# Three small experts' products placed between the weight units of the five large ones, and the branch for further slots moved behind the experts

## The chip, the core and the metric

The kernel runs on one core of a Trainium2 chip. Its engines run side by side and wait for each other through semaphores: TensorE (PE in the rows, its weight loads PEld), VectorE (DVE), ScalarE (ACT), GpSimd (POOL) and SyncE (SP), which here issues the loads of weights. The metric is the device time of one execution in microseconds, lower is better.

## What is computed

Two transformer blocks of two layers each, over 256 tokens of width 1024, in float32. The change concerns one place, the mixture of experts in the second layer of the first block. A router picks 2 of 8 experts for each token, and each expert is a gated MLP of inner width 3584:

```python
logits = (xt @ w_router).astype(jnp.float32)
top_v, top_e = lax.top_k(logits, TOP_K)
gates = jax.nn.softmax(top_v, axis=-1)
...
def _swiglu(x, w1, w3, w2):
    return (jax.nn.silu(x @ w1) * (x @ w3)) @ w2
```

The output of an expert is scaled by its gate and added to the rows of its tokens.

## The kernel before

All weights go through one `Stream`. A load fetches 1 MiB (128 partitions x 2048 floats) into one of four raw buffers, issued by SP in the order of `Stream.loads`. `Stream.need` (L322 on) splits a raw tile into a high part `wh` (ACT, L338) and a low part `wl` (DVE, L339), each of two k-tiles of 128 rows by 512 columns; six pairs of such buffers exist (`SPLIT_BUFS`). `Thread.gemm` takes a split unit (two k-tiles) and issues three matmuls of 512 columns for each k-tile: L390 and L392 with `wh`, L391 with `wl`. All use the whole array of TensorE, 128 by 128. When a raw tile is split, `Stream.free` issues the next load.

Routing (`routing`) ranks the experts by their number of tokens. The five largest (`BIG`) get 128 slots each and run in `expert128`: for each of seven chunks of 512 inner columns a `gemm` with w1 and one with w3 of 8 k-tiles, then two `gemm` with w2 of 28 k-tiles, which is 42 loads and 3 x (7 x 2 x 8 + 2 x 28) = 504 matmuls for one expert. The inner activations are transposed on PE (L594), and the result is scattered back to the tokens by eight matmuls (L1611, L1612) and added to `XA` on DVE (`add_rows`).

The three smallest experts get 64 slots and run in `expert64` on the raw float32 weights, without splitting. `Thread.gemm_pair` computes two products side by side: a load holds two k-tiles of w1 and two of w3 in two transfers of 512 KB (for w2: two column chunks), and one half of the array's columns takes the first, the other half the second:

```python
for j in range(sk):
    k = k0 + j
    for c in range(2):
        m.nc.tensor.matmul(ps[c * 64:c * 64 + 64, :n], xT(k), w[:, c, j, :], start=(k == 0),
                           stop=(k == kc - 1))
m.stream.free(li)
```

So a load of a small expert is one unit of four matmuls of 64 by 512 (L407), and there are 42 units for each. A float32 matmul shows as two records in the trace. The raw buffer is held until PE has read it.

`moe` runs the eight experts one after the other in the order of ranks 0, 5, 1, 6, 2, 7, 3, 4 (`ORDER`). In the first of them a few loads come as halves into spare tiles (`raws`). `gather` and `gather64` collect an expert's tokens while the one before runs. Ahead of the first expert stands `overflow`: every engine loads the largest excess count into a register and branches (L1672, L1684); its body runs only when an expert has more tokens than slots, and on these inputs it is skipped. After the last expert come a layer norm (BN_AGGR and what follows on DVE) and the second block, which starts with PE transposes of its result.

The order in which instructions stand on each engine is set by a scheduler when the program is built; PE runs its matmuls in that order.

Of the kernel before, what the change touches and what calls it, by code (L numbers as in the profile page):

```python
# [29 lines left out]
SM_N = 2  # L30
SM_END = 7
TOA = 3
TOB = 3
SMALL_AT = 1
# [16 lines left out]
ORDER = (0, 5, 1, 6, 2, 7, 3, 4)  # L51
# [85 lines left out]
def weight_plan():  # L137
# [3 lines left out]
    def add(key, name, idx, c0, c1, small=0):  # L141
        out.append((key, name, idx, c0, c1, small))
# [8 lines left out]
    for i in range(2):  # L151
# [17 lines left out]
        if i == 0:  # L169
            for ci, (a, b) in enumerate(chunks(2816)):  # L170
                add(("f1", ci), "dense_w1", (0,), a, b)
                add(("f3", ci), "dense_w3", (0,), a, b)
            full("f2", "dense_w2", (0,), D)
        else:
            for e in range(8):
                for ci in range(7):
                    small = [SM_N if SMALL_AT <= 7 * e + ci < SM_END else 0 for j in range(2)]
                    add((e, "e1", ci), "expert_w1", (0, e), ci * 512, ci * 512 + 512, small[0])
                    add((e, "e3", ci), "expert_w3", (0, e), ci * 512, ci * 512 + 512, small[1])
                full((e, "e2"), "expert_w2", (0, e), D)  # L180
# [26 lines left out]
def weight_groups(shapes):  # L207
# [5 lines left out]
    for key, name, idx, c0, c1, small in weight_plan():  # L213
# [9 lines left out]
        out.append((key, name, idx, c0, n, kc, small, g))  # L223
# [3 lines left out]
def packed_weights(h):  # L227
# [3 lines left out]
    for key, name, idx, c0, n, kc, small, groups in plan:  # L231
# [4 lines left out]
    return packs  # L236


class Stream:


    def __init__(self, m):
# [7 lines left out]
        self.owed = 0  # L250
        self.pin = True
# [3 lines left out]
    def add(self, key, name, n, kc, small, groups, rank=None):  # L255
        per = part_rows(n)
        lst = []
        for at, k, rows in groups:
            lk = per if len(lst) < small else rows
            for j in range(0, rows, lk):  # L260
                li = len(self.loads)
                self.loads.append(([(name, at, rows, j, lk, n)], lk < rows, rank))
                kk = 0
                while kk < lk:
                    sk = min(per, lk - kk)
                    lst.append(len(self.splits))
                    self.splits.append((li, kk, sk, k + j + kk, n, kc, kk + sk == lk))
                    kk += sk
        assert key not in self.index
        self.index[key] = lst  # L270

    def add_pair(self, key, chunks, kc, rank):

        lst = []
        for g in range(len(chunks[0][2])):
            k, rows = chunks[0][2][g][1:]
            for j in range(0, rows, 2):
                li = len(self.loads)
                self.loads.append(([(name, gr[g][0], rows, j, 2, n) for name, n, gr in chunks], False, rank))
                lst.append(len(self.splits))  # L280
                self.splits.append((li, None, 2, k + j, 512, kc, True))
        assert key not in self.index
        self.index[key] = lst

    def load(self, parts=1):
        while self.next_load < len(self.loads):
            li = self.next_load
            pieces, small, rank = self.loads[li]
            if rank is not None and rank not in self.m.expert:
                self.owed += 1  # L290
                return
            self.next_load += 1
            if small:
                r = self.m.A([P, 1024], F32, name="raws")
            else:
                r = self.m.praw.tile([P, 2048], F32, name="raw", tag="raw")
            for i, (name, at, rows, j0, lk, n) in enumerate(pieces):
                v = r[:, i * lk * n:(i + 1) * lk * n].rearrange("p (k n) -> p k n", k=lk)
                if rank is None:
                    src = self.m.I[name][at:at + P * rows * n].rearrange("(p k n) -> p k n", p=P, k=rows)  # L300
                else:
                    w = self.m.I[name].rearrange("(e q) -> e q", e=8)
                    src = w[bass.ds(self.m.expert[rank], 1), at:at + P * rows * n].rearrange(
                        "a (p k n) -> p (a k) n", p=P, k=rows)
                q = lk // parts
                for j in range(0, lk, q):
                    self.m.nc.sync.dma_start(v[:, j:j + q], src[:, j0 + j:j0 + j + q])  # L307
            self.raw[li] = r if len(pieces) > 1 else v
            if not small:
                return  # L310
# [9 lines left out]

    def need(self, idx):
        m = self.m  # L322
        nc = m.nc
        while self.next_split <= min(idx, len(self.splits) - 1):
            j = self.next_split
            li, kk, sk, k0, n, kc, last = self.splits[j]
            if li not in self.raw:
                return
            self.next_split += 1
            if kk is None:  # L330
                self.ready[j] = self.raw[li].rearrange("p (c k n) -> p c k n", c=2, k=sk)
                continue
# [16 lines left out]
    def free(self, li):  # L349
        del self.raw[li]  # L350
        if not self.loads[li][1]:
            self.load()


class Thread:
# [40 lines left out]
    def gemm_pair(self, key, xT):  # L396

        m = self.m
        ps = m.pmm.tile([P, 512], F32, name="mm", tag="mm")
        for s in m.stream.index[key]:  # L400
            yield s
            li, _, sk, k0, n, kc, _ = m.stream.splits[s]
            w = m.stream.ready.pop(s)
# [15 lines left out]
class Model:  # L419
# [108 lines left out]
    def run_one(self, g):  # L528
        for s in g:
            if isinstance(s, int):  # L530
                self.stream.need(s + SPLIT_BUFS - 2)
                self.stream.next_use = s + 1
                self.side_tick()

# [102 lines left out]
    def plan(self):  # L637
# [3 lines left out]
        for key, name, idx, c0, n, kc, small, groups in weight_groups(SHAPES)[0]:  # L641
            if not name.startswith("expert_"):
                S.add(key, name, n, kc, small, groups)
                continue
            if idx[1] > 0:
                continue
            one[key[1:] if key[1] in ("e1", "e3") else ("e2", key[1])] = (name, n, kc, small, groups)
            if ("e2", 1) not in one:
                continue
            for i, r in enumerate(ORDER):  # L650
                if r < BIG:
                    for k, (nm, nn, kk, sm, gr) in one.items():
                        S.add((r,) + k, nm, nn, kk, sm if i == 0 else 0, gr, r)
                else:
                    for ci in range(8):
                        ab = [one["e1", ci], one["e3", ci]] if ci < 7 else [one["e2", 0], one["e2", 1]]
                        S.add_pair((r, ci), [(nm, nn, gr) for nm, nn, _, _, gr in ab], ab[0][2], r)
# [721 lines left out]
    def routing(self):  # L1379
# [48 lines left out]
        reg(ORDER[0])  # L1428
        self.stream.pay()
        for r in ORDER[1:]:  # L1430
# [29 lines left out]
        yield from self.gather(ORDER[0])  # L1460
# [7 lines left out]
    def gather(self, r):  # L1468
# [3 lines left out]
        s = self.kvt([P, 2, P], name="oh")  # L1472
# [7 lines left out]
        if r == ORDER[0]:  # L1480
# [44 lines left out]
    def gather64(self, r):  # L1525
# [3 lines left out]
        s = self.kvt([P, 2, 2, 64], name="oh")  # L1529
# [9 lines left out]
        sT = []  # L1539
        for h in range(2):  # L1540
            d = self.kvt([P, 2, P], F32R, name="ohT")
            nc.scalar.activation(d, tp[:, 0:2, :], AF.Copy, scale=half[h])
            sT.append(d)
# [14 lines left out]
    def moe(self):  # L1558
        nc, I = self.nc, self.I
        th = Thread(self)  # L1560
        self.drain(self.route)
        self.xbs = self.pc.tile([P, 2, 4, 6], F32, name="xbs")
        self.overflow()
# [540 lines left out]
```

## Time and profile before

| | |
|---|---|
| time, median of 3 runs | 3048.02 us (3045.64 to 3055.02) |
| time of the profiled execution | 3051.97 us |
| its span, first to last instruction | 3050.2 us |
| mean granted clock of TensorE | 0.993 of full speed |
| busy: PE, DVE, ACT | 97%, 64%, 50% of the span |
| moved by DMA | 721.53 MB, 237 GB/s on the mean |
| experts: first matmul on gathered tokens to last scatter | 772.7 to 1747.2 us |

The time is about the span plus 2 us around it. A record of PE is longer than the distance to the next, since matmuls overlap in the pipeline; what a matmul costs is read from the distance between starts. "Idle before" in brackets is the time in which the engine had nothing running, with the event that ended it. In the table of stages each row is a stretch of the span, with the busy time of each engine, the granted clock, the busy share of the 16 DMA engines and the rate.

### The profile page before, as it was taken

The numbers are of one execution on the slowest core, as the hardware profiler recorded it, in microseconds if no ns is written. First come the engines' busy times: TensorE is split into PE (matmuls) and PEld (weight loads), VectorE is DVE, ScalarE is ACT, GpSimd is POOL, SyncE is SP. The second block draws the span as 40 slices with busy tenths as digits, with TensorE's granted clock in tenths as the row PEclk, the third lists the DMA queues.
The fourth block names the chain that finished last, engine by engine and source line by source line (L and its number), as shares of the span: only waits on it lengthen the run. The fifth ranks groups of instructions, "written<-read, shape, count | busy, mean of one in ns | idle before, by whom it ended". The sixth has DMA issues, their size and how long they took to land.

```text
span 3050.2 us, 38360 instructions
## 1 busy us (share of the span) xinstructions
PE 2954.7 (97%) x14208; PEld 2273.5 (75%) x14208; DVE 1958.3 (64%) x3240; ACT 1536.7 (50%) x2162; POOL 30.7 (1%) x47
## 2 busy tenths in 40 slices
PE   8999999999899998998999899999999999999998
PEld 6888887888762672572477778888888888888887
DVE  6877555777860771581488965757865655668655
ACT  4665444664750651470377644564454444654543
POOL 0000000000000000000000000000000000000000
PEclk9999999999999999999999999999999999999999
DMA  6445554443989999999999955545555555555553
GB/s 226 152 160 193 183 179 174 165 156 114 377 330 398 365 342 388 377 346 376 384 341 353 362 188 179 196 160 186 177 186 185 185 188 193 171 174 184 180 182 108
DMA packets 124769, 721.53 MB, mean 237 GB/s; under 512 B 14168, under 2 KB 14432, under 8 KB 59168
## 3 DMA queue, kind: packets, MB, share of 16 engines
q1 hardware_dynamic: 120096, 703.54, 63.8%
q0 software_dynamic: 4480, 15.48, 1.5%
q8 instruction: 113, 1.85, 0.2%
q14 instruction: 80, 0.66, 0.1%
HBM read 716.87 MB, written 2.10 MB: 236 GB/s over the span
## 4 chain that ended last, share of the span: by engine, by line
PE 61%; DMA 9%; DVE 3%; issue 1%; ACT 1%; SPq 0%; ACTq 0%; POOLq 0%; DVEq 0%
PE mm L391 18%; PE mm L392 18%; PE mm L390 18%; DMA raw<-in_expert_w_dram 8%; PE mm L407 3%; PE tp L594 2%; DVE wl L339 2%; DMA rows<-xrows,toki 1%; ACT wh L338 1%; PE tp L621 0%; PE rop L2017 0%; SPq L307 0%; PE ps L1854 0%; DVE z L1576 0%; PE pops L1022 0%
## 5 line engine op out<-in xcount | busy, mean ns | idle before, releaser
L339 DVE TENSOR_TENSOR wl<-raw,wh 128x1024 fp32r<-128x1024 f32 (+1 forms) x1064 | 1272.3, 1215 | 613.2 <-ACT wh L338 608.8
L338 ACT CAST wh<-raw 128x1024 fp32r<-128x1024 f32 (+1 forms) x1064 | 1088.3, 1046 | 771.2 <-PE mm L392 679.3
L390 PE MATMUL mm<-wh,tg 128*128 128x512 f32 (+2 forms) x2928 | 1142.3, 390 | 0.3 <-ACT tg L600 0.2
L391 PE MATMUL mm<-wl,tg 128*128 128x512 f32 (+2 forms) x2928 | 1120.9, 383 | 2.4 <-DVE wl L339 2.2
L392 PE MATMUL mm<-wh,tg 128*128 128x512 f32 (+2 forms) x2928 | 1122.2, 384 | 0.0
L392 PEld LDWEIGHTS mm<-wh,tg 128*128 128x128 f32 x2928 | 552.0, 189 | 109.1 <-DVE tg L604 1.2
L391 PEld LDWEIGHTS mm<-wl,tg 128*128 128x128 f32 x2928 | 553.2, 189 | 106.5 <-DVE wl L339 7.4
L390 PEld LDWEIGHTS mm<-wh,tg 128*128 128x128 f32 x2928 | 552.7, 189 | 102.3 <-issue 1.7
L390 PE MATMUL mm<-wh,xe 128*128 128x512 f32 x560 | 223.5, 399 | 10.1 <-DVEq L1684 10.1
L391 PE MATMUL mm<-wl,xe 128*128 128x512 f32 x560 | 224.1, 400 | 8.1 <-DVE wl L339 7.7
L392 PE MATMUL mm<-wh,xe 128*128 128x512 f32 x560 | 220.5, 394 | 0.0
L407 PE MATMUL mm<-raw,xs 128*64 128x512 f32 x672 | 187.6, 605 | 15.4 <-DMA raw<-in_expert_w_dram 14.3
L407 PEld LDWEIGHTS mm<-raw,xs 128*64 128x64 f32 x672 | 52.5, 136 | 136.2 <-DMA raw<-in_expert_w_dram 69.1
L391 PEld LDWEIGHTS mm<-wl,xe 128*128 128x128 f32 x560 | 106.1, 190 | 43.2 <-DVE wl L339 22.1
L390 PEld LDWEIGHTS mm<-wh,xe 128*128 128x128 f32 x560 | 106.1, 190 | 32.3 <-issue 10.5
L392 PEld LDWEIGHTS mm<-wh,xe 128*128 128x128 f32 x560 | 105.9, 189 | 21.0
L1639 DVE TENSOR_TENSOR h<-sl,mm 64x512 f32<-64x512 f32 x21 | 14.5, 691 | 165.4 <-ACT sl L1638 165.4
L600 ACT CAST tg<-tp 128x512 fp32r<-128x512 f32 (+1 forms) x127 | 64.4, 515 | 108.9 <-PE tp L594 108.3
L407 PE MATMUL mm<-raw,hT 128*64 128x512 f32 x336 | 101.0, 609 | 7.5 <-DMA raw<-in_expert_w_dram 6.9
L1638 ACT ACTIVATE sl<-mm 64x512 f32<-64x512 f32 x21 | 12.4, 588 | 179.7 <-PE mm L407 179.7
L601 DVE TENSOR_TENSOR tg<-tp,tg 128x512 fp32r<-128x512 f32 (+1 forms) x127 | 75.4, 600 | 23.3 <-ACT tg L600 21.2
L407 PEld LDWEIGHTS mm<-raw,hT 128*64 128x64 f32 x336 | 27.6, 135 | 78.2 <-DMA raw<-in_expert_w_dram 49.7
(394 smaller groups left out, 1940.3 us busy)
## 6 DMA issues: line engine op xcount, KB each, us to landing
raw<-in_expert_w_dram SPq DMA_DIRECT2D x198, 1024.0 KB, 6.9
raw<-in_expert_w_dram SPq DMA_DIRECT2D x252, 512.0 KB, 7.6
raw<-in_w_in_dram SPq DMA_DIRECT2D x101, 1024.0 KB, 4.8
raw<-in_ffn_w_in_dram SPq DMA_DIRECT2D x88, 1024.0 KB, 4.9
raw<-in_ffn_w_out_dram SPq DMA_DIRECT2D x40, 1024.0 KB, 4.9
raw<-in_dense_w_dram SPq DMA_DIRECT2D x32, 1024.0 KB, 4.9
raw<-in_w_out_dram SPq DMA_DIRECT2D x16, 1024.0 KB, 5.1
raws<-in_expert_w_dram SPq DMA_DIRECT2D x24, 512.0 KB, 12.9
```

The costliest lines, as they stand in the source:

```text
L338: i1 = nc.scalar.copy(hv, src)
L339: i2 = nc.vector.tensor_tensor(out=lv, in0=src, in1=hv.bitcast(F32), op=OP.subtract)
L390: nc.tensor.matmul(o, xh, wh[:, j, :], start=(k == 0), stop=False)
L391: nc.tensor.matmul(o, xh, wl[:, j, :], start=False, stop=False)
L392: nc.tensor.matmul(o, xl, wh[:, j, :], start=False, stop=(k == kc - 1))
L407: m.nc.tensor.matmul(ps[c * 64:c * 64 + 64, :n], xT(k), w[:, c, j, :], start=(k == 0), stop=(k == kc - 1))
L594: nc.tensor.transpose(tp[:, j, :], src[:, (k0 + j) * P:(k0 + j + 1) * P], self.ident)
L600: nc.scalar.copy(hi, tp[:, :nk, :])
L601: nc.vector.tensor_tensor(out=lo, in0=tp[:, :nk, :], in1=hi.bitcast(F32), op=OP.subtract)
L1638: nc.scalar.activation(sl[64:P, :], ps[0:64, :], AF.Silu)
L1639: nc.vector.tensor_tensor(out=h[odd * 64:odd * 64 + 64, :], in0=sl[64:P, :], in1=ps[64:P, :], op=OP.mult)
```

## The change

The five large experts now run one after the other (`larger`), the three small ones likewise (`smaller`), and `run_merged` steps whichever of the two generators has the earlier unit in one common stream. `add_experts` lays that stream: the loads of the large experts are numbered 0 to 209, the 126 loads of the small ones are spread evenly from place 12 to 20 before the end, and a large load is issued 2.5 places ahead of its use. The products of the small experts go to a PSUM tile of the pool `aux` (`pair`). The half loads (`raws`) are gone. Before the first gather has ended, only one unit of expert weights may be split (`hold`). `overflow` moves behind the experts; its body reloads the token rows and takes the statistics of the layer norm again. The one-hot of a gather moves to another pool. Cut to its core:

```diff
-ORDER = (0, 5, 1, 6, 2, 7, 3, 4)
+SMALL_FROM = 12
+SMALL_TO = 20
+SPLIT_LEAD = 2.5
...
+        step = (len(big) - SMALL_FROM - SMALL_TO) / len(small)
+        work, load = [], []
+        for i, x in enumerate(big):
+            load.append((i - SPLIT_LEAD, x))
+            work += [(i + j / len(x[3]), x, u) for j, u in enumerate(x[3])]
+        for i, x in enumerate(small):
+            load.append((SMALL_FROM + i * step, x))
+            work += [(SMALL_FROM + i * step, x, u) for u in x[3]]
...
+        self.hold = len(self.splits) + 1
...
-            if li not in self.raw:
+            if li not in self.raw or j == self.hold:
                 return
...
-        ps = m.pmm.tile([P, 512], F32, name="mm", tag="mm")
+        ps = m.aux(name="pair")
...
+    def run_merged(self, gens):
+
+        cur = [next(g, None) for g in gens]
+        while any(c is not None for c in cur):
+            i = min((c, i) for i, c in enumerate(cur) if c is not None)[1]
+            self.stream.need(self.stream.ahead(cur[i], SPLIT_BUFS - 2))
+            self.stream.next_use = cur[i] + 1
+            self.side_tick()
+            cur[i] = next(gens[i], None)
...
         yield
-        yield from self.gather(ORDER[0])
+        yield from self.gather(0)
+        self.stream.hold = None
...
         self.xbs = self.pc.tile([P, 2, 4, 6], F32, name="xbs")
+        self.gathers = {BIG: self.gather_side(BIG)}
+        self.run_merged([self.larger(), self.smaller()])
         self.overflow()
-        self.lnf = [self.bcast(I["ln_ffn_g"][1]), self.bcast(I["ln_ffn_b"][1])]
-        for i, r in enumerate(ORDER):
-            nxt = ORDER[i + 1] if i < 7 else None
-            yield from (self.expert128 if r < BIG else self.expert64)(th, r, nxt)
-        th.flush()
```

How the built program's order moves, at three places. The first is PE, at the start of the first small expert; before, `xs` is that expert's gathered tokens and L1611, L1612 scatter the large expert ahead of it:

```order
L390 MATMUL mm<-wh,tg 128x512
L391 MATMUL mm<-wl,tg 128x512
L392 MATMUL mm<-wh,tg 128x512
L407 MATMUL mm<-raw,xs 64x512 x8
L1611 MATMUL scp<-y,ohT 128x512
L1612 MATMUL scp<-y,ohT 128x512
L407 MATMUL mm<-raw,xs 64x512 x4
L1611 MATMUL scp<-y,ohT 128x512
L1612 MATMUL scp<-y,ohT 128x512
L407 MATMUL mm<-raw,xs 64x512 x21
```

In the changed program (lines 420 to 422 are what 390 to 392 were, 437 what 407 was; `xe` is the large expert's tokens), the third unit of the first small expert and the fourth's beginning:

```order
L437 MATMUL pair<-raw,xs 64x512
L420 MATMUL mm<-wh,xe 128x512
L421 MATMUL mm<-wl,xe 128x512
L422 MATMUL mm<-wh,xe 128x512
L420 MATMUL mm<-wh,xe 128x512
L437 MATMUL pair<-raw,xs 64x512 x3
L421 MATMUL mm<-wl,xe 128x512
L422 MATMUL mm<-wh,xe 128x512
L420 MATMUL mm<-wh,xe 128x512
L421 MATMUL mm<-wl,xe 128x512
L422 MATMUL mm<-wh,xe 128x512
L420 MATMUL mm<-wh,xe 128x512
```

Before, the units of a small expert stand in unbroken runs of up to 55 matmuls. Now each of the 126 units is broken in two, everywhere in the same way: its first matmul (first half of the columns) stands alone, then mostly four full-array matmuls, then the other three. So 252 runs of 64-column matmuls lie between full-array ones.

The second place is ACT at the start of the experts (`xe` is the high part of the first expert's tokens, `wh` of its weights, `pe` belongs to the work before). Before:

```order
L1492 CAST ohT<-ohp 128x256
L338 CAST wh<-raw 128x1024 x2
L1304 ACTIVATE pe<-mm 128x512
L338 CAST wh<-raw 128x1024 x4
L1495 CAST xe<-gp 128x512 x2
L1672 TENSOR_LOAD cmax
L1684 COMPARE_AND_BRANCH
```

and now:

```order
L1525 CAST ohT<-ohp 128x256
L1528 CAST xe<-gp 128x512
L369 CAST wh<-raw 128x1024
L1528 CAST xe<-gp 128x512
L369 CAST wh<-raw 128x1024
L1334 ACTIVATE pe<-mm 128x512
L369 CAST wh<-raw 128x1024 x6
```

The tokens' casts stand ahead of all splits but one, and the branch is gone from here. The third place is DVE behind the last expert, where the branch now stands between the last statistics (`xbs`) and the layer norm that uses them:

```order
L1618 SCALAR_TENSOR_TENSOR z_7092<-scp,rtab,z_7092 128x512
L1618 SCALAR_TENSOR_TENSOR z_7207<-scp,rtab,z_7207 128x512
L1623 BN_STATS xbs<-z_7092 128x6 x2
L1623 BN_STATS xbs<-z_7207 128x6 x2
L1717 TENSOR_LOAD cmax
L1730 COMPARE_AND_BRANCH
```

Before, BN_AGGR followed the statistics at once. SP has the same branch there, behind six loads of the next block.

## Rows read from the trace of the kernel before

**Rows 1.** Stages by window, experts of rank 0, 5, 1 and 4, and their sum
```profile
core 0: us, PE busy (x) PEld busy (x) DVE busy (x) ACT busy (x) POOL busy (x), PEclk, DMA share, GB/s
772.70:893.50 120.80, 120.67 (x539) 99.46 (x540) 104.18 (x103) 90.87 (x98) 1.23 (x1) 0.98 0.93 358
893.50:1006.90 113.40, 103.34 (x380) 31.79 (x378) 11.20 (x20) 10.89 (x18) 1.49 (x2) 1.00 0.98 385
1006.90:1136.00 129.10, 124.66 (x549) 97.74 (x549) 111.99 (x112) 89.62 (x101) 2.60 (x1) 1.00 0.94 349
...
1619.00:1747.20 128.20, 126.61 (x558) 100.31 (x556) 114.91 (x112) 93.26 (x104) 0.00 (x0) 1.00 0.95 359
sum 974.50, PE 923.71 PEld 586.20 DVE 588.98 ACT 485.71 POOL 12.70; mean PE 115.46 PEld 73.28 DVE 73.62 ACT 60.71 POOL 1.59
```

**Rows 2.** Timeline of PE in the small expert of rank 5: start, length, instruction, count
```profile
908.42 2.35 PE L407 MATMUL mm<-raw,xs 128*64 128x512 f32 x8 [0.21 <-DMA raw<-in_expert_w_dram]
910.98 2.35 PE L407 MATMUL mm<-raw,xs 128*64 128x512 f32 x8 [0.21 <-DMA raw<-in_expert_w_dram]
```

**Rows 3.** Waits from 772 to 1748 us: who for whom, total, times, longest
```profile
PEld mm L407 <- DMA raw<-in_expert_w_dram: 118.9, 158, 2.4
```

**Rows 4.** Timeline of PE, first and last of 39 full-array matmuls in a row
```profile
1736.06 0.39 PE L390 MATMUL mm<-wh,tg 128*128 128x512 f32 x1
...
1744.69 0.39 PE L392 MATMUL mm<-wh,tg 128*128 128x512 f32 x1
```

**Rows 5.** Timeline of PE, a lone 64-column matmul between full-array ones
```profile
1131.10 0.39 PE L390 MATMUL mm<-wh,tg 128*128 128x512 f32 x1
1131.42 1.07 PE L407 MATMUL mm<-raw,xs 128*64 128x512 f32 x2
1132.42 0.50 PE L391 MATMUL mm<-wl,tg 128*128 128x512 f32 x1
1132.76 0.39 PE L392 MATMUL mm<-wh,tg 128*128 128x512 f32 x1
1132.99 0.39 PE L390 MATMUL mm<-wh,tg 128*128 128x512 f32 x1
```

**Rows 6.** Timeline of PE, a unit's last three matmuls between transposes, then three units running on
```profile
958.59 1.93 PE L407 MATMUL mm<-raw,xs 128*64 128x512 f32 x6
960.45 0.77 PE L594 MATMUL tp<-c,rows 128*128 128x128 f32 x5
...
961.14 5.37 PE L407 MATMUL mm<-raw,xs 128*64 128x512 f32 x24
966.34 1.02 PE L407 MATMUL mm<-raw,hT 128*64 128x512 f32 x2
```

**Rows 7.** DMA issues: tile, count, KB each, median us to landing
```profile
raw<-in_expert_w_dram SPq DMA_DIRECT2D x198, 1024.0 KB, 6.9
```

**Rows 8.** Timeline of PE at the start of the experts
```profile
762.25 0.40 PE L392 MATMUL mm<-wh,tg 128*128 128x512 f32 x1
772.70 0.76 PE L390 MATMUL mm<-wh,xe 128*128 128x512 f32 x1 [10.05 <-DVEq L1684]
773.26 0.63 PE L391 MATMUL mm<-wl,xe 128*128 128x512 f32 x1
```

**Rows 9.** Timeline of ACT at the same place
```profile
767.86 1.99 ACT L338 CAST wh<-raw 128x1024 fp32r<-128x1024 f32 x2 [2.64 <-DMA raw<-in_expert_w_dram]
769.76 1.06 ACT L1495 CAST xe<-gp 128x512 fp32r<-128x512 f32 x2
```

**Rows 10.** The branch ahead of the experts: sequencer records of its load and jump, ns
```profile
L1672 DVEq TENSOR_LOAD <-cmax x1: 546/546/546, 770.9 to 770.9; - x1
...
L1684 PEldq COMPARE_BRANCH  x1: 6392/6392/6392, 760.4 to 760.4; - x1
...
L1684 DVEq COMPARE_BRANCH  x1: 72/72/72, 771.5 to 771.5; - x1
```

**Rows 11.** Timeline of PE behind the last expert
```profile
1746.48 0.73 PE L1612 MATMUL scp<-y,ohT 128*128 128x512 f32 x2
1755.89 1.30 PE L594 MATMUL tp<-c,xln 128*128 128x128 f32 x5 [8.68 <-DVE xln L1060]
```

More of the change, by code (lines that the diff above doesn't have):

```diff
@@ L272, in add_pair @@
[L272 to L283, printed above, removed]
@@ L285, in load @@
-    def load(self, parts=1):
[L286 to L294, printed above, removed]
-            else:
[L296 to L310, printed above, removed]
@@ new lines, in unit, with add, add_experts @@
+    def unit(self, key, li, kk, sk, k0, n, kc, last):
+        self.index.setdefault(key, []).append(len(self.splits))
+        self.splits.append((li, kk, sk, k0, n, kc, last))
+    def add(self, key, name, n, kc, groups):
+        assert key not in self.index
+        for pieces, units in chunk_loads(name, n, kc, groups):
+            self.loads.append((pieces, None))
+            for u in units:
+                self.unit(key, len(self.loads) - 1, *u)
+    def add_experts(self, one):
+        big, small = [], []
+        for r in range(8):
+            if r < BIG:
+                for k, (name, n, kc, groups) in one.items():
+                    big += [((r,) + k, r, pieces, units) for pieces, units in chunk_loads(name, n, kc, groups)]
+            else:
+                for ci in range(8):
+                    ab = [one["e1", ci], one["e3", ci]] if ci < 7 else [one["e2", 0], one["e2", 1]]
+                    small += [((r, ci), r, pieces, units) for pieces, units in pair_loads(ab)]
+        step = (len(big) - SMALL_FROM - SMALL_TO) / len(small)
[6 more added lines that the diff above has]
+            work += [(SMALL_FROM + i * step, x, u) for u in x[3]]
+        li = {}
+        for _, x in sorted(load, key=lambda a: a[0]):
+            li[id(x)] = len(self.loads)
+            self.loads.append((x[2], x[1]))
+        self.hold = len(self.splits) + 1
+        for _, x, u in sorted(work, key=lambda a: a[0]):
+            self.unit(x[0], li[id(x)], *u)
@@ new lines, in load @@
+    def load(self, parts=1):
+        if self.next_load == len(self.loads):
+            return
+        li = self.next_load
+        pieces, rank = self.loads[li]
+        if rank is not None and rank not in self.m.expert:
+            self.owed += 1
+            return
+        self.next_load += 1
+        r = self.m.praw.tile([P, 2048], F32, name="raw", tag="raw")
+        for i, (name, at, rows, j0, lk, n) in enumerate(pieces):
+            v = r[:, i * lk * n:(i + 1) * lk * n].rearrange("p (k n) -> p k n", k=lk)
+            if rank is None:
+                src = self.m.I[name][at:at + P * rows * n].rearrange("(p k n) -> p k n", p=P, k=rows)
+            else:
+                w = self.m.I[name].rearrange("(e q) -> e q", e=8)
+                src = w[bass.ds(self.m.expert[rank], 1), at:at + P * rows * n].rearrange(
+                    "a (p k n) -> p (a k) n", p=P, k=rows)
+            q = lk // parts
+            for j in range(0, lk, q):
+                self.m.nc.sync.dma_start(v[:, j:j + q], src[:, j0 + j:j0 + j + q])
+        self.raw[li] = r if len(pieces) > 1 else v
@@ L319, in start, with ahead @@
             self.load()
+    def ahead(self, j, n):
+        while n and j + 1 < len(self.splits):
+            j += 1
+            n -= self.splits[j][1] is not None
+        return j
     def need(self, idx):
@@ L350, in free @@
         del self.raw[li]
-        if not self.loads[li][1]:
-            self.load()
+        self.load()
 class Thread:
@@ L640, in plan @@
         one = {}
-        for key, name, idx, c0, n, kc, small, groups in weight_groups(SHAPES)[0]:
+        for key, name, idx, c0, n, kc, groups in weight_groups(SHAPES)[0]:
             if not name.startswith("expert_"):
[L643 to L649, printed above, removed]
-            for i, r in enumerate(ORDER):
[L651 to L657, printed above, removed]
+                S.add(key, name, n, kc, groups)
+            elif idx[1] == 0:
+                one[key[1:] if key[1] in ("e1", "e3") else ("e2", key[1])] = (name, n, kc, groups)
+                if ("e2", 1) in one:
+                    S.add_experts(one)
     def setup(self):
```

125 lines of the change are left out of this document (70 added, 55 removed).

## The prediction

> **What bounds the kernel now.** I read the table of stages first. The experts take 974.5 us of the span, and the stages are of two kinds [rows 1]. With a large expert TensorE is busy nearly all the time (120.67 of 120.80 us in the first), and the DMA engines move 349 to 359 GB/s. With a small one TensorE looks busy too (103.34 of 113.40 us), VectorE and ScalarE do next to nothing, and DMA is at 385 GB/s and a busy share of 0.98. The timeline of TensorE tells what the small stage waits for: the units start 2.56 us apart, and each start is released by a load [rows 2]; the table of waits sums this to 118.9 us over the three small experts, with a longest wait of 2.4 us [rows 3]. A unit is 1 MiB, so a small stage is bounded by its loads. A large stage is bounded by TensorE, at almost the rate at which its loads arrive. The change lets the loads of the small experts use TensorE's long stretches. What it can give is the waiting of the small stages; what it can cost is on TensorE, since that engine decides once the loads no longer do.
>
> **TensorE's work, priced from rows.** A full-array matmul of 512 columns takes (1744.69 - 1736.06) / 38 = 0.227 us of the queue [rows 4]. A unit of a small expert that stands in a run takes (966.34 - 961.14) / 3 = 1.73 us: eight records, which start two by two, one for each half of the columns, every 1.73 / 4 = 0.43 us [rows 6].
>
> The order of the changed program never lets a unit stand in a run. All 126 units are broken into one matmul and three, with full-array ones around both. The trace of before happens to hold such a place. From 1131.10 to 1132.99 us there are three full-array distances, 0.68 us, and one lone 64-column matmul [rows 5]: it costs 1.89 - 0.68 = 1.21 us. Of that 2 x 0.43 = 0.87 us is its own stream, with the other half of the columns idle, and 0.34 us are lost at its two edges: it starts late, and the full-array matmuls on both sides of its end are 1.00 and 0.34 us apart. The three others take two steps of two records and two of one, 4 x 0.43 = 1.73 us, plus the same edges, 2.07 us; the row of such a three between transposes shows 1.86 us from its start to the next instruction, without the edge ahead [rows 6]. So a broken unit costs 1.21 + 2.07 = 3.28 us of TensorE, and one that runs on costs 1.73.
>
> The Trainium skill, "TensorEngine Tiling (Array Packing)", section "Tiling Modes", states that changing the tiling mode drains TensorE while changing tiles within a mode does not, which speaks against this change. If I price that drain alone by the overhang of a full-array record (0.39 us long, 0.23 apart [rows 4], so 0.16 at each of two edges), a broken unit would cost 3.24 us and the sum below would be 5 us lower; the row of the lone matmul agrees with the rule to that extent, and its 0.34 us stands in the sum.
>
> A large expert without waits takes 120.8 us in the first stage; that has about 2.4 us too much for the half-speed start (clock 0.98 of 120.8 us [rows 1]) and lacks its own 8 scatter matmuls, 1.8 us, which fall in the next stage: 120.2 us. For a small expert I add to its 42 units 22 transposes at some 0.12 us and 8 scatter matmuls at 0.227 us, together 4.5 us. TensorE's sum is 5 x 120.2 + 3 x (42 x 3.28 + 4.5) = 601 + 427 = **1028 us**, against 974.5 us that the stages take now with all their waits. With unbroken units it would be 601 + 3 x (42 x 1.73 + 4.5) = 833 us.
>
> **The loads.** 8 experts x 42 loads of 1 MiB are 352.3 MB. Over 1028 us that is 343 GB/s, under what the large stages get (349 to 359) and well under the small ones' 385. So TensorE decides, and DMA no longer ends the waits. Some are left where both meet. Bounds: nothing, as in the first large stage, and 129.1 - 120.2 = 8.9 us for a large expert as in the third row [rows 1], 7% or 72 us over the whole. A load lands 6.9 us after its issue [rows 7], while four raw buffers cover some 4 x 1028 / 336 = 12 us of TensorE's work, and six split units lie behind them. I take 10 us, near the lower end, because a late load now meets a slower consumer. The removed half loads only served the first stage; their bytes come as whole loads, at no cost of their own. The DVE, ACT and POOL work of the experts is the same as before and has more time; their busy sums of 589, 486 and 13 us [rows 1] lie beside TensorE's.
>
> **The start.** TensorE stands 10.05 us ahead of the first expert [rows 8]. The release is DVE's branch, but what comes last there are the gathered tokens: ScalarE casts them at 769.76, behind a split that waited for the third load until 767.86 [rows 9]. Now the casts stand ahead of those splits, and only one split is allowed before. TensorE can go on close to 763 us, which gives the 10 us and most of the 2.4 us of half speed. But the third load is not earlier, and TensorE takes 12 x 0.227 = 2.7 us for one, so some 4 us come back as waits: **-8 us**, bounds -4 and -12. Of the gathers, queued on POOL, none is moved past another's data; their results are needed tens of microseconds later.
>
> **The end.** The branch now lies on DVE's chain from the last scatter to the layer norm, for which TensorE waits 8.68 us already [rows 11]. DVE's load of the count took 0.55 us and its jump 0.07 us [rows 10], part of it while the engine still worked. Queued behind it are the layer norm and, on SP, three loads: SP waits until all loads in flight have landed, but the raw and split buffers then hold several loads of the next block, more than TensorE can use in that time. PE's jump took 6.39 us [rows 10], partly draining; it fits in the 8.68. **+1 us**, bounds 0 and +7, the upper one if DVE's jump takes as long as PE's did.
>
> The Trainium skill, "Runtime: NRT & Kernel Launch", section "Instruction fetch mechanics", says that a taken branch outside the prefetched window stalls its engine for a fetch. By that, DVE would pay it too, and the end would cost up to the 6.4 us that PE's row shows; DVE's own row, 0.07 us, does not show it.
>
> **The sum.** 1028 + 10 - 974.5 - 8 + 1 = +56.5 us. Against the profiled execution's own 3051.97 us this is 3108.5; that execution lies 3.95 us above the median of the runs, 3048.02, from which I forecast **3105 us**. Its own range: no waits, the whole start and nothing at the end give 1028 - 974.5 - 12 = +41.5, and 5 us of error in the edges 3085; 50 us of waits, a start of -4 and an end of +7 give +106, 3155.
>
> **Rivals.**
> *The broken units cost nothing: faster.* If the lone matmul ran beside its full-array neighbours, or its edges were waits of that one place, TensorE would need about 833 us and the loads decide: 352.3 MB at the small stages' 385 GB/s are 915 us, with 10 us of waits 925. That gives 925 - 974.5 - 8 + 1 = -56.5 us, 2992. For it: the small stages' waits are real and large. Against it: the lone matmul's row has no wait in it, its second record ends just where the next instruction starts, and the order is fixed when the program is built. It would take a unit price under 1.73 + (3.28 - 1.73) x (974.5 - 833) / (1028 - 833) = 2.85 us for the experts merely to break even. Chance 0.08.
> *The raw buffers decide: slower still.* A small load now holds one of four raw buffers until TensorE has reached both of its parts, and large loads pass through the same four. If the loads fall under 343 GB/s, the buffers take over from TensorE; at 320 GB/s the experts take 1101 us and the time is 3048 + 1101 - 974.5 - 7 = 3168 us. For it: the later large stages get only 349 GB/s and lose 8 us each to late splits. Against it: they ask for 120.2 us an expert, faster than the new stage. Chance 0.11.
> *The change does not do what it says, or gain and cost cancel.* The order shows the units of both kinds interleaved from the first to the last small unit, so this needs a cost half way: 3048. Chance 0.03.
>
> **How the numbers follow.** The forecast has 0.78. What a measurement of this kernel can tell from no change is about 0.3%, 9 us. Both the forecast and the buffers' rival are slower by more: 0.89. The faster rival gives 0.08, the rest 0.03. The range for 8 in 10 is the forecast's own, 3085 to 3155, with a little at the upper end for the buffers' rival near it: 3083 to 3158.
>
> **What would show it.** Right: a single stretch of the experts of some 1040 us with TensorE busy over 97% throughout and DMA at about 340 GB/s; pairs of records of the lone matmul followed by a full-array one about 1.0 us after its first start; waits of weight loads on DMA down from 118.9 us to a few; a first expert matmul near 763 us. Wrong: a stretch under 960 us, or four steps of two records in a unit; or long waits of TensorE on raw tiles, which would be the buffers.

## The result, and the profile after

The changed kernel takes 3206.39 us (median of 4 runs, 3203.03 to 3209.92) against 3049.22 us for the kernel before on the same chip: a ratio of 1.0514, 95% interval 1.0491 to 1.0536. It is slower, as forecast, but by 157 us where 56.5 were worked out, and it lies outside the range.

The profiled execution of the change has a span of 3201.8 us. The experts run from 758.4 us to 1899.3 us, 1141 us instead of 974.5. Five equal stretches of that, in the table of stages of the changed kernel (columns as in [rows 1]):

```profile
758.40:986.60 228.20, 206.18 (x757) 117.77 (x756) 125.35 (x137) 104.58 (x123) 4.41 (x4) 0.97 0.84 308
986.60:1214.70 228.10, 212.22 (x731) 109.88 (x730) 109.88 (x111) 87.04 (x100) 0.95 (x1) 0.96 0.84 299
1214.70:1442.90 228.20, 213.22 (x766) 111.66 (x765) 112.05 (x118) 93.38 (x110) 3.03 (x3) 0.99 0.86 312
1442.90:1671.00 228.10, 219.38 (x784) 115.28 (x783) 114.79 (x116) 95.56 (x109) 2.89 (x4) 0.99 0.91 329
1671.00:1899.30 228.30, 215.08 (x809) 126.69 (x807) 134.98 (x133) 107.42 (x120) 0.55 (x1) 1.00 0.89 325
```

TensorE has idle time in every stretch (22 us in the first), its granted clock is 0.97 and 0.96 of full speed on the mean of the two stretches in which it idles most, and the loads run at 299 to 329 GB/s, below every large stage before. No engine is full. That is the picture of engines that wait for each other in turn.

**What a broken unit costs** is seen in the timeline of PE of the changed kernel, here the lone matmul and the three others of one unit:

```profile
896.32 0.39 PE L422 MATMUL mm<-wh,tg 128*128 128x512 f32 x1
896.64 1.07 PE L437 MATMUL pair<-raw,xs 128*64 128x512 f32 x2
897.64 0.50 PE L420 MATMUL mm<-wh,tg 128*128 128x512 f32 x1
...
898.44 0.40 PE L420 MATMUL mm<-wh,tg 128*128 128x512 f32 x1
898.76 1.93 PE L437 MATMUL pair<-raw,xs 128*64 128x512 f32 x6
...
900.62 0.50 PE L421 MATMUL mm<-wl,tg 128*128 128x512 f32 x1
```

From the full-array matmul ahead to the one behind there are 1.32 and 2.18 us, and over the 126 units the medians are 1.32 and 2.19. Less one full-array distance (0.227), plus 0.11 because the next full-array matmul follows after 0.34, that is 1.20 + 2.07 = 3.27 us. The prediction had 1.21 + 2.07.

**The split of the time.** For each run I add up the distances between neighbouring starts on PE in the experts as they are where nothing waits: 0.227 us between full-array matmuls (0.34 for the first behind half-array ones), 0.109 between transposes, 1.32 across a lone 64-column matmul, 2.19 across three or four of them, 1.73 for each further unit in a run. That is "own". What the stage has beyond it is "waits", with what a lower clock costs included: by the clock in the rows above, at most some 20 us of the change's 120.

| run | time, us | experts, us | own | waits |
|---|---|---|---|---|
| before | 3049.22 | 974.5 | 837 | 138 |
| the change | 3206.39 | 1141.0 | 1021 | 120 |
| e1_whole | 3093.66 | 1029.0 | 871 | 158 |
| e2_buf5 | 3211.85 | 1146.1 | 1021 | 125 |
| e3_whole_buf5 | 3073.54 | 1010.7 | 871 | 140 |
| e4_blocks | 3057.69 | 998.0 | 847 | 151 |
| e5_act | 3172.76 | 1116.6 | 1021 | 96 |
| e8_act_buf5 | 3174.75 | 1110.3 | 1021 | 89 |
| e6_pe | 3123.85 | 1051.2 | 914 | 137 |
| e7_pe_buf5 | 3052.65 | 990.5 | 914 | 77 |
| e9_gather | 3021.82 | 956.2 | 913 | 44 |
| e10_all | 2982.80 | 918.1 | 871 | 47 |
| e11_front | 2987.98 | 916.9 | 871 | 46 |
| e12_raw4 | 3076.42 | 1013.3 | 871 | 143 |

The change adds 184 us of own work, about as forecast, and keeps nearly all the waits, which was not. They have moved. Before, 99.5 of the 138 us stood ahead of small units, which waited for loads, and 30 at the large experts' matmuls. Now 10 stand ahead of small units, 79 at large matmuls, 17 ahead of the transposes of gathered rows (6 before) and 12 ahead of those of h.

**What they wait for.** From the table of waits of the changed kernel, 758 to 1900 us (total, times, longest, with rows left out; [rows 3] is its counterpart, and that row is gone):

```profile
DVE wl L370 <- ACT wh L369: 205.9, 92, 16.0
ACT wh L369 <- DMA raw<-in_expert_w_dram: 190.4, 74, 6.9
...
ACT sl L1684 <- PE pair L437: 151.5, 21, 9.1
...
ACT tg L640 <- PE tp L634: 101.8, 31, 8.8
...
ACT sl L1634 <- PE mm L422: 73.7, 19, 8.8
...
PEld mm L421 <- DVE wl L370: 51.1, 54, 2.4
...
PEld mm L420 <- ACT wh L369: 40.9, 32, 2.1
```

TensorE waits for splits, the splits wait for ScalarE, and ScalarE waits for two things: for blocks that have not landed, and for TensorE itself (the silu of a pair and of a large chunk, copies of transposes). The timeline shows one such circle, PE, ACT and DVE together:

```profile
1051.30 0.59 ACT L640 CAST tg<-tp 128x512 fp32r<-128x512 f32 x1 [2.78 <-PE tp L634]
...
1056.93 0.39 PE L422 MATMUL mm<-wh,xe 128*128 128x512 f32 x1
1057.36 0.60 ACT L1634 ACTIVATE sl<-mm 128x512 f32<-128x512 f32 x1 [5.46 <-PE mm L422]
1057.85 2.93 ACT L369 CAST wh<-raw 128x1024 fp32r<-128x1024 f32 x3
1058.92 2.36 DVE L370 TENSOR_TENSOR wl<-raw,wh 128x1024 fp32r<-128x1024 f32 x2 [6.30 <-ACT wh L369]
1058.94 0.19 PEld L420 LDWEIGHTS mm<-wh,xe 128*128 128x128 f32 x1 [2.04 <-ACT wh L369]
1058.94 0.49 PE L420 MATMUL mm<-wh,xe 128*128 128x512 f32 x1 [1.62 <-ACT wh L369]
```

ScalarE stands idle for 5.46 us, because the next instruction in its queue is the silu of a chunk that TensorE is still working on. Behind the silu stand three splits, which then run without a gap: their blocks were there. TensorE ends the chunk at 1056.93 and can only go on when the silu and the first of those splits are through, 2.01 us from start to start instead of 0.227. In the order of the changed program, 13 of the 41 evacuations of a large chunk (silu or y) that lie among small units have no later split ahead of them on ScalarE; the program's text emits four splits ahead of each, and the scheduler, which sets the final order, put them behind.

How much of the 120 us is of this kind can be read from the same trace, by following each wait of TensorE back from releaser to releaser to the first instruction that stood waiting. Some 75 us begin with an instruction of ScalarE or VectorE that waits for TensorE: the silu and y of large chunks (24 and 8 us), the silu of small ones (14), VectorE's product h of large chunks (15) and its additions of scattered rows (9), copies of transposes (5). Rows of a gather that land late begin 16 us, a late block of weights less than 1: ScalarE's 190.4 us of waiting for blocks hardly reaches TensorE directly. Some 15 us are the lower clock, and the rest is too short to follow. Split buffers do not run short: ScalarE waits under 7 us in all for one to be given back. This is a reading of one trace; the experiments test a part of it. The row of the gathers, from the groups of PE (busy time and mean ns, then the idle time before and what ended it):

```profile
L661 PE MATMUL tp<-c,rows 128*128 128x128 f32 x12 | 3.2, 380 | 15.1 <-DMA rows<-xrows,toki 15.1
```

**Start and end**, in the timeline of PE of the change:

```profile
758.16 0.39 PE L422 MATMUL mm<-wh,tg 128*128 128x512 f32 x1
758.39 0.39 PE L420 MATMUL mm<-wh,xe 128*128 128x512 f32 x1
...
1898.61 0.73 PE L1655 MATMUL scp<-y,ohT 128*128 128x512 f32 x2
1908.26 1.30 PE L634 MATMUL tp<-c,xln 128*128 128x128 f32 x5 [8.91 <-DVE xln L1090]
```

The wait ahead of the first expert [rows 8] is gone, and behind the last scatter TensorE waits 8.91 us where it waited 8.68 [rows 11]: the branch at the end costs 0.2 us at most.

### The profile page after: what moved, and what is told of

It reads as the page before. It is cut to its first block, busy times and chain, and to the rows that moved or that the text cites. A ratio compares the mean times of both kernels' runs of the same rounds, so it can differ in the third digit from the quotient of the medians.

```text
span 3201.8 us, 38250 instructions
## 1 busy us (share of the span) xinstructions
PE 3093.1 (97%) x14208; PEld 2265.8 (71%) x14208; DVE 1958.9 (61%) x3240; ACT 1533.8 (48%) x2161; POOL 28.8 (1%) x47
## 5 line engine op out<-in xcount | busy, mean ns | idle before, releaser
L370 DVE TENSOR_TENSOR wl<-raw,wh 128x1024 fp32r<-128x1024 f32 (+1 forms) x1088 | 1299.1, 1215 | 772.9 <-ACT wh L369 770.4
L369 ACT CAST wh<-raw 128x1024 fp32r<-128x1024 f32 (+1 forms) x1088 | 1110.0, 1044 | 915.1 <-PE mm L422 664.1
L437 PE MATMUL pair<-raw,xs 128*64 128x512 f32 x672 | 253.7, 614 | 0.0
L420 PE MATMUL mm<-wh,xe 128*128 128x512 f32 x560 | 231.4, 413 | 21.1 <-ACT wh L369 21.1
L421 PE MATMUL mm<-wl,xe 128*128 128x512 f32 x560 | 234.4, 419 | 16.8 <-DVE wl L370 16.4
L422 PE MATMUL mm<-wh,xe 128*128 128x512 f32 x560 | 227.1, 406 | 0.0
L437 PEld LDWEIGHTS pair<-raw,xs 128*64 128x64 f32 x672 | 55.9, 135 | 106.2 <-issue 106.0
L437 PE MATMUL pair<-raw,hT 128*64 128x512 f32 x336 | 126.7, 613 | 0.0
L1685 DVE TENSOR_TENSOR h<-sl,pair 64x512 f32<-64x512 f32 x21 | 14.5, 690 | 124.4 <-ACT sl L1684 124.4
L1684 ACT ACTIVATE sl<-pair 64x512 f32<-64x512 f32 x21 | 12.4, 591 | 151.5 <-PE pair L437 151.5
L1637 DVE TENSOR_TENSOR h<-sl,mm 128x512 f32<-128x512 f32 x35 | 24.0, 686 | 79.9 <-PE mm L422 79.7
```

Of the source, the lines that this page charges most:

```text
L369: i1 = nc.scalar.copy(hv, src)
L370: i2 = nc.vector.tensor_tensor(out=lv, in0=src, in1=hv.bitcast(F32), op=OP.subtract)
L420: nc.tensor.matmul(o, xh, wh[:, j, :], start=(k == 0), stop=False)
L421: nc.tensor.matmul(o, xh, wl[:, j, :], start=False, stop=False)
L422: nc.tensor.matmul(o, xl, wh[:, j, :], start=False, stop=(k == kc - 1))
L1637: nc.vector.tensor_tensor(out=h, in0=sl, in1=ps, op=OP.mult)
```

## The experiments

Two theories at first. A: the broken units decide, their price is the difference. B: the four raw buffers decide, since a block's mean stay in a buffer, 13.45 us in the change's trace (12.65 for large blocks before), over four gives 3.36 us a block, 336 blocks, 1130 us. That product is no evidence for B by itself: where each load is issued when a buffer comes free, it gives the length of the stage whatever sets it. In e2_buf5, with five buffers, the mean stay is 17.0 us, and 336 x 17.0 / 5 is 1142 us again.

**e1_whole.** The change with the four matmuls of a small unit kept together on TensorE:

```diff
-                for c in range(2):
-                    m.nc.tensor.matmul(ps[c * 64:c * 64 + 64, :n], xT(k), w[:, c, j, :], ...)
+                for c in (1, 0):
+                    with ExitStack() as cx:
+                        if first is not None:
+                            cx.enter_context(m.tc.issue_after(first))
+                        i = m.nc.tensor.matmul(ps[c * 64:c * 64 + 64, :n], xT(k), w[:, c, j, :], ...)
+                    first = first or i.ins
```

> The four matmuls of each small unit stand together on TensorE (2.07 us instead of 1.21 + 2.07). Theory A, the price of the broken units decides and the waits beside it stay: 152 us less, 3054 us. Theory B, the rotation of four raw buffers decides (each load is issued 0.03 us after the buffer four loads earlier is freed; stage = 336 x mean hold / 4, and the hold was 13.1 us for a large and 14.0 for a small load): the hold of a small load falls to about 11 us and that of a large one to about 12.6, the stage to 1009 us and the time to 3075 us, with loads still issued the moment a buffer is freed. Under 2990 us neither holds.

**e2_buf5.** The change with five raw buffers, paid for with two of the 23 slots:

```diff
-RAW_BUFS = 4
+RAW_BUFS = 5
-SLOTS = 23
+SLOTS = 21
```

> Five raw buffers instead of four, 21 spare tiles instead of 23, units broken as in the change. A: the waits come from elsewhere, 3206 us within 15. B: the waits of TensorE on splits go, the experts come near TensorE's own sum of 1028 us, some 1050, and the time is about 3116 us.

**e3_whole_buf5.** Both.

> Both. A: as with whole units alone, 3054 us. B: TensorE's sum is 876 us, the loads at the 385 GB/s of the small stages 915, with some waits 935 us; time about 3000 us, below the kernel before.

**e4_blocks.** All of the change but the interleaving: the units of a small expert stand in one block behind a large one.

```diff
-            load.append((SMALL_FROM + i * step, x))
-            work += [(SMALL_FROM + i * step, x, u) for u in x[3]]
+            at = 42 * (1 + i // 42) - 0.5 + i % 42 / 100
+            load.append((at, x))
+            work += [(at, x, u) for u in x[3]]
```

> The change with the units of each small expert in one block behind a large expert, as before the change: everything else of it (branch at the end, start, PSUM tile, no half loads) stays. If the interleaving alone costs the time (A and B): experts about 975 us and 3206 - 1140 + 975 = 3041 us. If something else of the change does (the branch, the PSUM pool, the dropped half loads): over 3100 us.

Measured: 3093.66 us (ratio 1.0145, interval 1.0127 to 1.0163), 3211.85 (1.0537, 1.0511 to 1.0564), 3073.54 (1.0069, 1.005 to 1.0089) and 3057.69 (1.0024, 1.0014 to 1.0034). e4_blocks has the other parts of the change and nearly the old time, so the loss is the interleaving's. Breaking the units costs 113 us: a whole unit has the same 2.19 us from neighbour to neighbour as the three alone, so 126 x 1.2 = 150 us of own work go, but 38 us come back as waits. B falls as it was stated: a fifth buffer did nothing to the change. A falls too: with whole units 158 us of waits are left, and neither theory said why a stage with 871 us of work and loads that can come in under 920 takes 1029: both runs with whole units came out some 20 us or more above what either theory gave.

The timeline above gave the next theory. C: the order of the in-order queues makes the waits; an instruction that waits for TensorE stands ahead of work that could be done. D: the transfers bound the stage at these rates, whatever the order.

**e5_act.** The change; on ScalarE the silu and the y of a large chunk stand behind the splits that were emitted before them (the call adds an edge of order alone, to the engine's previous instruction in the text):

```diff
-            nc.scalar.activation(sl, ps, AF.Silu)
+            self.tc.keep_in_program_order(nc.scalar.activation(sl, ps, AF.Silu))
...
-            nc.scalar.copy(y[:, 0, :], ps)
+            self.tc.keep_in_program_order(nc.scalar.copy(y[:, 0, :], ps))
```

> Only ScalarE's order is changed: of the large experts the silu and the copy of y stand behind the four splits that the program has emitted by then (in the change 13 of 41 stand ahead of every later split, now 2). The broken units stay. Theory C (the waits of the changed kernel come from ScalarE's queue: an evacuation that waits for TensorE stands ahead of splits whose block has landed): the groups of waits that begin with the silu or with y, 27.6 and 12.0 us in the changed kernel's trace, go: 3166 us. Theory D (the waits come from the transfers, which come late at 309 to 345 GB/s, whatever the order of the queues): 3206 us.

**e6_pe.** The change; on TensorE every matmul of a small unit, and the first of each three of a large one, keeps the order of the text:

```diff
-                    m.nc.tensor.matmul(ps[c * 64:c * 64 + 64, :n], xT(k), w[:, c, j, :], ...)
+                    m.tc.keep_in_program_order(
+                        m.nc.tensor.matmul(ps[c * 64:c * 64 + 64, :n], xT(k), w[:, c, j, :], ...))
...
-                nc.tensor.matmul(o, xh, wh[:, j, :], start=(k == 0), stop=False)
+                i = nc.tensor.matmul(o, xh, wh[:, j, :], start=(k == 0), stop=False)
+                if pin:
+                    m.tc.keep_in_program_order(i)
```

> TensorE's matmuls of the experts keep the order in which the program emits them: each small unit stands whole and at its own place, some four large units earlier than the scheduler puts it; ScalarE then has 4 to 6 splits ahead of nearly every evacuation. Theory C: the broken units' price goes (about 150 us, as the stage's pure sum falls from 1028 to some 878) and of the 113 to 150 us of waits some 60 to 110 go too: 2990 us, faster than before. Theory D: as with whole units alone, 3094 us, or 3075 at best.

**e7_pe_buf5.** e6_pe with five raw buffers and 21 slots.

> The same with five raw buffers (and 21 instead of 23 slots). Theory C: with the queues' order mended a late block is what is left, and a fifth buffer takes some 10 us more: 2980 us. Theory D: 3070 us, as whole units with five buffers.

Measured: 3172.76 us (1.0405, 1.0388 to 1.0423), 3123.85 (1.0257, 1.0234 to 1.028) and 3052.65 (1.0014, 1.0004 to 1.0023).

e5_act gives 34 us by the medians and 27 between the profiled spans (3201.8 and 3175.1), near what C had. Followed back as above, the waits that begin with the silu and y of large chunks fall from 24 and 8 us (the expectation counts 27.6 and 12.0) to 5 and 1, and those that begin with VectorE's additions from 9 to 4; the other groups stay about where they were, and the waits for rows grow from 17 to 26. So the order of ScalarE's queue alone is shown to cost some 30 us.

e6_pe is a miss for both theories: slower than e1_whole, although the waits at large matmuls fell from 111 us there to 8. The waits of the small units are back. From its table of waits, 759 to 1811 us:

```profile
ACT wh L369 <- PE mm L424: 227.2, 173, 6.8
...
PEld pair L440 <- DMA raw<-in_expert_w_dram: 71.3, 66, 3.3
ACT wh L369 <- DMA raw<-in_expert_w_dram: 69.5, 44, 5.1
```

ScalarE now waits above all for split buffers that TensorE has yet to free (the first row): it is ahead. But a small unit, which the scheduler had placed some four large units later than the text, now comes at its place, before its block has landed: 71.3 us. There the fifth buffer counts: e7_pe_buf5 is 71 us faster than e6_pe, and that row falls to 11.8 us. Its time, 3052.65 us, still lies nearer to D's 3070 than to C's 2980. What is left at TensorE in e7_pe_buf5 is led by the gathers, by its table of PE's waits:

```profile
PE tp L637 <- DMA rows<-xrows,toki: 17.6, 3, 6.7
...
PE tp L664 <- DMA rows<-xrows,toki: 5.4, 2, 3.4
```

**e8_act_buf5.** e5_act with five raw buffers, to see whether the buffer counts with ScalarE's order alone (E: it counts only where TensorE takes the small units at their place).

> Broken units as in the change, ScalarE's order mended as in e5_act, and five raw buffers. Buffers alone gave nothing (e2_buf5), ScalarE's order 34 us (e5_act), and with TensorE's order kept the fifth buffer gave 71 us (e7_pe_buf5 against e6_pe). If the fifth buffer counts as soon as no evacuation stands in the splits' way (theory C), 3140 us; if it counts only where small units stand at their own place on TensorE, so that their blocks are awaited there (theory E), 3173 us.

**e9_gather.** e7_pe_buf5 with

```diff
-GATHER_WAIT = 4
+GATHER_WAIT = 10
```

> e7_pe_buf5 with the transposes of the gathered rows ten steps behind the gather's issue instead of four, so that the rows have landed (7.2 to 9.5 us after the issue) when TensorE comes to them. In e7_pe_buf5 TensorE waits some 26 us for rows. Theory C, in which each in-order wait on TensorE counts in full: 3027 us. If another wait takes its place (theory D: the transfers bound the stage): 3053 us.

**e10_all.** e9_gather with the experts' transposes and scatter matmuls in the text's order too:

```diff
+    def pinned(self, i):
+        return self.tc.keep_in_program_order(i) if self.pin else i
...
-            nc.tensor.transpose(tp[:, j, :], src[:, (k0 + j) * P:(k0 + j + 1) * P], self.ident)
+            self.pinned(nc.tensor.transpose(tp[:, j, :], src[:, (k0 + j) * P:(k0 + j + 1) * P], self.ident))
...
+        self.pin = True
         self.run_merged([self.larger(), self.smaller()])
+        self.pin = False
```

> e9_gather with TensorE's transposes and scatters in the program's order too, so that no small unit is broken by one of them (159 runs of half-array matmuls become 126). The pure sum falls by some 33 runs of 1.1 us, 36 us: 2990 us by theory C, 3053 by theory D; if the pinned transposes now wait for the silu and the product ahead of them (41 chunks of some 1 us), 3030.

Measured: 3174.75 us (1.0414, 1.0398 to 1.043), 3021.82 (0.9908, 0.9895 to 0.9922) and 2982.8 (0.9786, 0.9772 to 0.9799). E holds for e8_act_buf5: the fifth buffer is worth nothing there. e9_gather gives 31 us where 26 were worked out, and e10_all another 39 where 36 were worked out. **e10_all beats both kernels**, the one before by 2.1%. In its timeline a unit stands whole, and its stages are another picture than the change's:

```profile
1205.52 0.39 PE L424 MATMUL mm<-wh,xe 128*128 128x512 f32 x1
1205.83 1.94 PE L440 MATMUL pair<-raw,xs 128*64 128x512 f32 x8
1207.70 0.50 PE L420 MATMUL mm<-wh,xe 128*128 128x512 f32 x1
```

```profile
760.20:943.80 183.60, 177.44 (x752) 113.12 (x752) 128.17 (x136) 107.31 (x124) 4.98 (x4) 1.00 0.99 390
943.80:1127.40 183.60, 182.40 (x771) 111.48 (x769) 116.65 (x117) 95.94 (x106) 1.92 (x1) 1.00 1.00 392
...
1311.10:1494.70 183.60, 183.55 (x769) 113.16 (x769) 117.48 (x119) 95.55 (x107) 2.55 (x4) 1.00 1.01 401
1494.70:1678.30 183.60, 180.46 (x773) 121.56 (x771) 128.72 (x125) 106.52 (x115) 0.55 (x1) 1.00 0.97 381
```

The DMA engines are busy throughout, at 381 to 401 GB/s, and TensorE's granted clock is 1.00. Of the 47 us of waits 31 stand ahead of small units again: the loads bound the stage now, which D had claimed for the change itself.

**e11_front.** e10_all with the branch for further slots ahead of the experts:

```diff
         self.xbs = self.pc.tile([P, 2, 4, 6], F32, name="xbs")
+        self.overflow()
...
         self.run_merged([self.larger(), self.smaller()])
...
-        self.overflow()
```

> e10_all with the branch for further slots back ahead of the experts, as in the kernel before. In the changed kernel's trace the experts' first matmul stood 14.3 us earlier than before (758.4 against 772.7) and TensorE's first transpose behind the last scatter was no later (9.3 against 9.4 us). If the whole of the earlier start is the branch's, some 14 us slower than e10_all: 2997 us; if the start is hidden by another wait of the first expert, 2983 us.

**e12_raw4.** e10_all with four raw buffers and 23 slots.

> e10_all with four raw buffers (and 23 slots). By e7_pe_buf5 against e6_pe the fifth buffer is worth 71 us once TensorE keeps the program's order; where TensorE's pure sum is lower still, the same or more: 3055 to 3065 us. If the fifth buffer was needed only because of broken units or late rows: 2990 us.

Measured: 2987.98 us (0.9801, 0.9777 to 0.9825) and 3076.42 (1.0085, 1.0061 to 1.0109). The branch's place is worth 5 us, not 14, and 5 us is little more than these runs tell apart: the two intervals against the kernel before overlap. The experts' start, by the timeline of PE in e11_front, is 7.1 us later than in e10_all (760.25), and behind this wait the granted clock is 0.50 until 771.0 us (0.63 us a record instead of 0.39):

```profile
767.39 0.76 PE L420 MATMUL mm<-wh,xe 128*128 128x512 f32 x1 [7.62 <-DVEq L1739]
767.95 0.63 PE L423 MATMUL mm<-wl,xe 128*128 128x512 f32 x1
```

From 772.7 us before to 767.4 here the gain must come from other edits than the branch; which one was not tried. In e12_raw4 the wait for small blocks returns, 94 us with one buffer less, and the time is 11 us above the expected range:

```profile
PEld pair L440 <- DMA raw<-in_expert_w_dram: 114.8, 102, 3.1
```

So neither order nor buffer does it alone: with the scheduler's order the fifth buffer gave nothing broken and 20 us whole, with the text's order 71 and 94 us.

## Why the prediction was wrong in size

**The price of a broken unit: right.** 1.20 + 2.07 us against 1.21 + 2.07, and 1021 us of own work against 1028. The Trainium skill, "TensorEngine Tiling (Array Packing)", section "Tiling Modes", states that changing the tiling mode drains TensorE. The rows agree: some 0.34 us are lost at the edges of each stretch of half-array matmuls. But the price could be avoided, which the prediction did not ask: a whole unit among large ones costs 2.07 (e1_whole).

**The step that failed is "I take 10 us".** The waits were 120 (113 beyond the prediction's own sum of 1028), above the bound of 72 as well. The reasons given for it were that four raw buffers cover 12 us, that six split units lie behind them, and that "a late load now meets a slower consumer". The runs showed that the cover was not where it was counted. It existed in the text, four splits ahead, but the final order of ScalarE's queue had taken it away at 13 of 41 chunk ends; giving it back gave some 30 us (e5_act). With it fails the sentence that the busy sums of the other engines "lie beside TensorE's": in the trace some 75 of the 120 us begin with an instruction of ScalarE or VectorE that waits for TensorE with other work queued behind it. Beyond the 30 us no run took these out alone, so for the rest the cause is read from the trace and not shown. Nor is the count of splits ahead all of it: in e1_whole no large chunk ends with fewer than two, and 158 us of waits are left. The gathers, of which the prediction said that their results are needed tens of microseconds later, were put at nothing and cost 17 us. The buffers were not what ran short at the change's order (e2_buf5, e8_act_buf5), so the rival with the raw buffers, 3168 us, came nearer to the time by luck, not by its own mechanism. That mechanism is real, but worth 20 us with whole units (e3_whole_buf5) and 71 and 94 only once TensorE meets the small units at their place (e7_pe_buf5, e12_raw4). The upper bound failed because it was taken from large stages in which an evacuation mostly has two splits ahead of it: no row of before held the new order, and the order of the changed program, which could be read, was priced for TensorE alone.

**The waits of before: half right.** The 118.9 us on loads [rows 3] did go, as forecast. That TensorE would then be busy over 97% throughout did not follow: the waits at the large matmuls rose from 30 to 79 us.

**Start and end.** The start gained 14.3 us instead of 8, the end cost 0.2 instead of 1. The 4 us priced for the late third load did not come: TensorE has no distance over 1 us between starts from 758.39 to 770.17 us. For a taken branch the Trainium skill, "Runtime: NRT & Kernel Launch", section "Instruction fetch mechanics", states that one whose target was not prefetched stalls its engine for a fetch. In the trace of the change PE's jump at the end takes 5.57 us and DVE's 0.07; whether PE's is such a stall no run shows, and it lies within the 8.91 us that TensorE waits there anyway.

Summed as the prediction did it: 1141.0 - 974.5 - 14.3 + 0.2 = +152.4 us between the two profiles (their spans differ by 151.6), of which +184 are own work, -18 waits and -14 the two ends. Of the remaining waits of the change 17 us are shown to be rows that come late, by their own row and by e9_gather in the mended order; those that begin with the small experts' silu (14 us), with VectorE's h and additions (15 and 9) and with copies of transposes (5) were not taken out one at a time. In e10_all, which keeps TensorE's order throughout and has a buffer more, all that begins with ScalarE or VectorE is down to some 10 us.

## What to carry to other kernels

Price a new order on every in-order queue, not only on the bounding engine: for each instruction that waits for that engine, count how much ready work stands ahead of it in the final order, since look-ahead in the text is no look-ahead where a scheduler moves instructions. When a buffer more changes nothing, that does not acquit the buffers; mend the order first and ask again. Matmuls of a narrower tile should stand together when they are placed among wide ones: the stretch pays its edges once, and here three cost as much as four.

## What the runs showed of the hardware

Three and four 64-column matmuls between full-array ones take the same 2.19 us (records of 1.93 and 1.94 us), as four start two by two and the third of three has no partner: in both the records start 0.33, 0.81, 1.24 and 1.67 us behind the full-array matmul ahead, two at a time but for the last two starts of the three. A lone one takes 1.32. And the loads, which gave 358 GB/s beside a large expert and 385 in a small one [rows 1], ran at 381 to 401 GB/s for 918 us beside a TensorE that was almost never idle (e10_all). With the same order and four buffers (e12_raw4) it was 355 GB/s on the mean of the experts: the lower rates were a matter of when and how many loads were issued, not of what the transfers can do beside the engines.
